# Strips of keys, a table on a 64-byte grid, first loads on two queues and a searched order in a one-core encoder layer

## The chip, the cores and the metric

The kernel runs on one core of a Trainium2 chip. The metric is device time in microseconds of one execution, as the median of several runs. The core has a matrix engine (TensorE, "PE" in the profile, whose weight loads are listed apart as "PEld"), three engines for elementwise work (VectorE "DVE", ScalarE "ACT", GpSimd "POOL") and SyncE ("SP"), which in the kernel before issues every DMA. The engines run at the same time and wait for each other by semaphores. Matmuls write into PSUM (8 banks of 128 x 512 float32), everything else lives in SBUF (128 partitions).

## The reference: what is computed

One encoder layer is applied to two sequences with the same weights: a "prompt" of 512 tokens and a "sample" of 1024 tokens, both 1024 wide, in float32. With `h = rms_norm(x)`:

```
u_pool, g_pool, q, k, v, g_attn = split(h @ w_in)          # 1024 -> 6 x 512
pool_out = pool_mixer(u_pool) * silu(g_pool)               # centred means over 2/4/8/16 tokens, 4 groups
q, k     = rms_norm per head (8 heads of 64), q / sqrt(64)
attn_out = neighbourhood_attention(q, k, v, rpb) * silu(g_attn)
y        = x + concat(pool_out, attn_out) @ w_out
```

The attention sees the tokens as a grid 64 columns wide: 16 rows in the sample, 8 in the prompt. A token attends to 8 rows by 16 columns around it, clamped at the borders; a learned bias per head depends on the row and column distance between query and key.

## The kernel before

**Numbers.** Operands of the large products are split into a high and a low part (`split`, `low`), and a product is three matmuls: high by high, high by low, low by high (`mm3`). The transposes of q, k and of the softmax weights are done on TensorE against an identity (`ident`).

**Stages.** The four pairs of heads are run one after the other, first for the sample (`ss`), then for the prompt (`pr`). For a pair p: `project_qkv` multiplies 128 tokens at a time by the pair's q, k, v columns (tile `acc`), normalises, writes v to DRAM (`vd`), and transposes q and k (bank `ptq`) into the tiles `q` and `k`, two token tiles (4 rows of the grid) at a time; `gate` and `u_block` make the gates and the input of the pooling (banks `accg`, `accu`); `attention` makes the pair's two heads; `pooling` the pool group. At the end the output projection (bank `acco`) reads the mixed activations back from DRAM, in part by a scheme with fewer products (`T`, `S`, `A`).

**Attention of the sample, before.** A head is 8 blocks of 128 queries: two halves of the grid (`rt`), 8 rows each, by four groups of 16 columns (`cb`). A block's keys are 12 rows by 32 columns, stored row by row; in the first and last column group only 24 of the 32 columns are multiplied (288 scores), in the others all (384). Per block: two matmuls make the scores (bank `s`, high and low part of k), DVE adds the bias and takes the maximum, ACT takes the exponential (`ns` or `ns_edge`), one of DVE and ACT normalises, three transposes (bank `pt`), a split into `pp`, three matmuls with v (bank `po`), and after every second block three DVE instructions and one of ACT fold the result into the gate `sg`. The bias tile is loaded from a table in DRAM (`tab`) by 13 DMAs a head, as the bias of a block depends on how its rows are clamped; v is loaded by 4 DMAs for every 4 rows, with columns that overlap between the groups. The prompt has 4 blocks a head with 8 rows of keys and two chunks.

**Order.** The program is not issued as written. Each call is recorded as an `Op`, and `Plan.order` is a list scheduler: it keeps a clock, a cost per operation (`cost`), one DMA pipe (`transfer`) and the rings of buffers, and at each moment starts on every free engine the ready operation with the lowest priority number, then the lowest sequence number. Work that waits for another engine gets `TO_PE = 800` ns on the way. Some operations may go to one of several engines (`choice`). The resulting order is fixed at build time, and each engine runs its list in that order.

**The start.** SP issues `g_sb` (the norm's weights), then x and the first weights chunk by chunk. The first projection takes four token tiles together (`group` 4 in `tok_blocks`); for chunk c of the 1024 inputs each of the four does its three matmuls.

Of the kernel before, what the change touches and what calls it, by code (L numbers as in the profile page):

```python
# [35 lines left out]
CT = (2, 1, 1, 0)  # L36
BANKS = dict(acc=3, s=2, pt=2, po=1)
# [6 lines left out]
class Plan:  # L44
# [4 lines left out]
    class Op:  # L49
        __slots__ = ("eng", "fn", "ns", "bytes", "pri", "seq", "need", "next", "alloc", "uses", "port", "half", "ways")  # L50
# [178 lines left out]
    def order(self):  # L229
        ops = self.ops  # L230
        wait = [len(op.need) for op in ops]
        for op in ops:
            for d in op.need:
                ops[d].next.append(op)
# [35 lines left out]
        while True:  # L270
            for eng, heap in ready.items():
                left_over = []
                while heap and not busy[eng]:
# [23 lines left out]
                    if op.bytes:  # L297
                        dma = max(dma, end + 650) + op.bytes
                        done = dma + 1300
                    heapq.heappush(events, (end, 0, op.seq))  # L300
# [26 lines left out]

    def issue(self):
        for _, op in self.order():
            op.fn()  # L330


TO_PE = 800
# [5 lines left out]
def encoder(ctx, tc, xn_p, xt_p, xn_s, xt_s, w_in, w_out, w_pool, pscale, ng, qg, kg,  # L339
# [23 lines left out]

    g_sb = sb.tile([P, KC], F32, name="g_sb")
    ident = sb.tile([P, P], F32, name="ident")
    qk_t = sb.tile([P, 2], F32, name="qk_t")
    gqk = sb.tile([P, 1], F32, name="gqk")
    psc = sb.tile([P, NPAIR], F32, name="psc")
    edge = sb.tile([P, NPAIR, 16], F32, name="edge")

    def late_consts():
        sp.dma_start(out=qk_t[:, 0:1], in_=qg)
        sp.dma_start(out=qk_t[:, 1:2], in_=kg)
        dve.scalar_tensor_tensor(out=gqk, in0=qk_t[:, 0:1], scalar=HD ** -0.5, in1=qk_t[:, 1:2],
                                 op0=ALU.mult, op1=ALU.mult)
        sp.dma_start(out=psc, in_=pscale)
        sp.dma_start(out=edge, in_=edge_d)

# [3 lines left out]
    tab = dram.tile([32, HR, 32], F32, name="tab")  # L382

    def build_table():
        rel = ring("pv", 1, [P, 80], "rel")
        sp.dma_start(out=rel[0:HR, 0:48], in_=rpbm.rearrange("h r c -> (h r) c"))
        sp.dma_start(out=rel[0:HR, 48:79], in_=rpb.rearrange("h r c -> (h r) c"))

# [14 lines left out]
    def bias_rows(out, h, ro, q0, nq, a):  # L403

        o = tab.offset + (h * 15 + ro) * 32
        if nq == 1:
            sp.dma_start(out=out[16 * q0:16 * q0 + 16, :, a:a + 256],
                         in_=bass.AP(tab.tensor, o, [[HR * 32, 16], [8 * HR * 32, 3], [1, 256]]))
            return
        for ct in range(3):  # L410
            sp.dma_start(out=out[16 * q0:16 * (q0 + nq), ct, a:a + 256],
                         in_=bass.AP(tab.tensor, o + ct * 8 * HR * 32, [[32, nq], [HR * 32, 16], [1, 256]]))

    def load_bias(bt, kind, h):
        if kind == "all":
            bias_rows(bt, h, 0, 0, 8, 0)
        elif kind == "top":
            bias_rows(bt, h, 3, 3, 5, 0)
            for q in range(3):
                bias_rows(bt, h, 3, q, 1, (3 - q) * 32)  # L420
        else:
            bias_rows(bt, h, 0, 0, 4, 128)
            for q in range(4, 8):
                bias_rows(bt, h, 3, q, 1, (7 - q) * 32)
# [63 lines left out]
    ns_edge = {cb: sb.tile([P, 384], F32, name=f"ns_edge_{cb}") for cb in (0, 3)}  # L488
    bias = [sb.tile([P, 3 * 384], F32, name=f"bias_{i}") for i in range(2)]
# [3 lines left out]
    class Sequence:  # L493


        def __init__(self, sq, S, kt_rows, hts, Rb):
            self.sq, self.S, self.kt_rows, self.hts, self.Rb = sq, S, kt_rows, hts, Rb
            self.NT, self.NB, self.CH, self.KEYS = S // P, S // 512, kt_rows // 4, kt_rows * 32
            self.mixed = dram.tile([KC, P, S], F32, name=f"mixed_{sq}")
            self.rr = sb.tile([P, self.NT], F32, name=f"rr_{sq}")  # L500
# [14 lines left out]

        def prep(self, raw, xt, b, c):

            sp.dma_start(out=raw, in_=xt[c * P:(c + 1) * P, b * 512:(b + 1) * 512])
            ht = self.hts[b][c]
            split(ht[:, 0], ht[:, 1], raw, g_sb[:, c:c + 1])  # L520
# [21 lines left out]
        def tok_blocks(self, accs, w, t0):  # L542
            with plan.priority(MAIN):
                for c in range(KC):
                    for t, acc in enumerate(accs, t0):
# [11 lines left out]
        def project_qkv(self, p, w, group=1):  # L557
# [3 lines left out]
            for t0 in range(0, self.NT, 2):  # L561
# [33 lines left out]
                for i, t in enumerate((t0, t0 + 1)):  # L595
# [7 lines left out]
                    pe.transpose(pt[:, i * P:(i + 1) * P], in_=qkv[:, 0:P], identity=ident)  # L603
                    pe.transpose(pt[:, 256 + i * P:256 + (i + 1) * P], in_=qkv[:, P:256], identity=ident)
# [4 lines left out]
                rt, r0 = (2 * t0) // 8, (2 * t0) % 8  # L609
                lo, hi = 7 - r0, 3 - r0  # L610
                qa = slice(base + rt * 512, base + (rt + 1) * 512)
                ka = slice(base + t0 * P, base + t0 * P + 256)
                own = [slice(hd * HD, hd * HD + HD) for hd in range(2)]
                k_src = [pt[own[hd], 256:512] for hd in range(2)]
                q_src = [pt[own[hd], 0:256].rearrange("p (r cb c) -> p r cb c", r=4, cb=4) for hd in range(2)]
                q_dst = []
                for hd in range(2):
                    for rows in (own[hd], own[1 - hd]):
                        v = q[hd][rows, qa].rearrange("p (cb r c) -> p r cb c", cb=4, r=8)
                        q_dst.append(v[:, lo::-1, :, ::-1] if hi < 0 else v[:, lo:hi:-1, :, ::-1])  # L620
                for hd in range(2):
                    for rows in (own[hd], own[1 - hd]):
                        act.activation(out=k[hd][rows, ka], in_=k_src[hd], func=AF.Copy, scale=gqk[own[hd]])
                    act.activation(out=q_dst[2 * hd], in_=q_src[hd], func=AF.Copy)
                for hd in range(2):
                    low(k[2 + hd][own[hd], ka], k_src[hd], k[hd][own[hd], ka], gqk[own[hd]])
                    low(q_dst[2 * hd + 1], q_src[hd], q_dst[2 * hd])
                rg = t0 // 2
# [15 lines left out]

        def attention(self, p):
            for hd in range(2):
                for rt in range(self.NB):
                    h = 2 * p + hd
                    kind, i = (("top", 0), ("bot", 1))[rt] if self.S == 1024 else ("all", h % 2)
                    bt = bias[i][:, 0:3 * self.KEYS].rearrange("p (t c) -> p t c", t=3)  # L650
                    load_bias(bt, kind, h)
                    self.head_rows(p, hd, rt, bt)

        def head_rows(self, p, hd, rt, bt):
            sq, KEYS, base = self.sq, self.KEYS, self.base(p)
            h, lo, rbase = 2 * p + hd, hd * HD, 4 * rt

            g = sg[lo:lo + HD, base + rt * 512:base + (rt + 1) * 512]
            for cb in range(4):
                nm = f"{sq}_{h}_{rt}_{cb}"  # L660
                s = bank("s", f"s_{nm}")
                qo = base + rt * 512 + cb * P

                c0, n = CK[cb]

                def kv(x):
                    return x[:, base:base + self.S].rearrange("p (r c) -> p r c", c=GW)[
                        :, rbase:rbase + self.kt_rows, C0[cb] + c0:C0[cb] + c0 + n]

                def seen(x):  # L670
                    return x.rearrange("p (r c) -> p r c", c=32)[:, :, c0:c0 + n]
                sv = s[:, 0:self.kt_rows * n]
# [401 lines left out]
```

## Time and profile before

| | us |
|---|---|
| median of 3 runs (lowest to highest) | 648.28 (647.86 to 649.45) |
| the profiled execution | 648.4 |
| its span, from the first to the last instruction | 646.6 |
| TensorE busy | 635.0 |
| VectorE busy | 557.1 |
| ScalarE busy | 372.8 |
| GpSimd busy | 100.6 |

A row of a group of instructions reads: line, engine, operation, output<-inputs, output and input shape, count | busy us, mean ns of one | idle time of the engine just before them and what ended it. All recorded operations carry the line of the helper that issues them, L330, so groups are told apart by the names of their tiles (s_s is the bank `s` of the sample, po_p the bank `po` of the prompt). [...]

### The profile page before, as it was taken

How to read it: one execution, taken by the hardware profiler on the slowest of the kernel's cores; microseconds unless marked ns; L12 is line 12 of the kernel's file. 1: busy time of each engine (PE TensorE's matmuls, PEld its weight loads, DVE VectorE, ACT ScalarE, POOL GpSimd, SP SyncE). 2: the span in 40 equal slices, each digit the busy share in tenths (PEclk: the TensorE clock that was granted, in tenths of full speed). 3: DMA queues.
4: the chain of work that ended last, by engine and by line, in shares of the span. 5: the costliest groups of instructions: out<-in, count | busy, mean ns of one | idle time of the engine just before them, and what ended most of it. 6: DMA issues, size and time to landing. Idle time of an engine off the chain costs nothing.

```text
span 646.6 us, 11390 instructions
## 1 busy us (share of the span) xinstructions
PE 635.0 (98%) x3404; PEld 567.0 (88%) x3404; DVE 557.1 (86%) x1647; ACT 372.8 (58%) x910; POOL 100.6 (16%) x142
## 2 busy tenths in 40 slices
PE   6999999999999999999999999999999999999997
PEld 5998899988899888999889989899899878887886
DVE  6688999899987999967999989989999989879742
ACT  5766786568656476544777556477566457323210
POOL 1130100000000000101001110021212423405412
PEclk9999999999999999999999999999999999999999
DMA  8974354442274522425344355545556687843631
GB/s 304 348 205 143 104 169 124 123 121 79 59 246 137 182 62 69 134 95 152 127 112 143 109 168 162 174 139 144 169 174 195 189 261 231 269 152 118 191 131 65
DMA packets 92961, 101.53 MB, mean 157 GB/s; under 512 B 12900, under 2 KB 78564, under 8 KB 92900
## 3 DMA queue, kind: packets, MB, share of 16 engines
q1 hardware_dynamic: 92900, 100.81, 50.7%
q8 instruction: 27, 0.44, 0.3%
q14 instruction: 34, 0.28, 0.1%
HBM read 81.41 MB, written 19.37 MB: 156 GB/s over the span
## 4 chain that ended last, share of the span: by engine, by line
PE 91%; DVE 4%; DMA 3%; issue 1%; ACT 0%; SPq 0%; DVEq 0%; ACTq 0%
PE acc_s L330 21%; PE acco L330 15%; PE accg_s L330 14%; PE acc_p L330 10%; PE accu_s L330 7%; PE accg_p L330 6%; PE po_s L330 4%; PE accu_p L330 3%; PE pt_s L330 3%; PE s_s L330 3%; DMA xr<-in_xn_s 1%; PE po_p L330 1%; PE ptq_s L330 1%; DVE B L330 1%; PE pt_p L330 1%
## 5 line engine op out<-in xcount | busy, mean ns | idle before, releaser
L330 PE MATMUL acc_s<-w_sA,ht_s 128*128 128x384 f32 x768 | 145.9, 342 | 6.3 <-DVE w_sA L330 6.3
L330 PEld LDWEIGHTS acc_s<-w_sA,ht_s 128*128 128x128 f32 x768 | 136.0, 190 | 7.6 <-ACT ht_s L330 5.9
L330 PE MATMUL accg_s<-ht_s,w_sT 128*128 128x512 f32 x384 | 100.4, 399 | 0.0
L330 PEld LDWEIGHTS accg_s<-ht_s,w_sT 128*128 128x128 f32 x384 | 70.0, 188 | 12.0
L330 PE MATMUL acc_p<-w_pA,ht_p 128*128 128x384 f32 x384 | 75.4, 339 | 0.7 <-DVE w_pA L330 0.5
L330 PEld LDWEIGHTS acc_p<-w_pA,ht_p 128*128 128x128 f32 x384 | 66.1, 188 | 1.8 <-DVE w_pA L330 0.8
L330 PE MATMUL acco<-B,left 128*128 128x512 f32 x228 | 56.2, 395 | 0.6 <-DVE left L330 0.6
L330 PE MATMUL accu_s<-ht_s,w_sT 128*128 128x512 f32 x192 | 53.0, 400 | 0.0
L330 PEld LDWEIGHTS acco<-B,left 128*128 128x128 f32 x228 | 41.9, 188 | 9.5 <-DVE left L330 1.0
L330 PE MATMUL accg_p<-ht_p,w_pT 128*128 128x512 f32 x192 | 47.6, 395 | 0.0
L330 PEld LDWEIGHTS accg_p<-ht_p,w_pT 128*128 128x128 f32 x192 | 35.3, 188 | 6.9
L330 ACT ACTIVATE k<-ptq_s,gqk 64x256 fp32r<-64x256 f32 x64 | 30.1, 470 | 18.8 <-PE ptq_s L330 18.1
L330 PEld LDWEIGHTS accu_s<-ht_s,w_sT 128*128 128x128 f32 x192 | 34.6, 188 | 5.1
L330 DVE TENSOR_TENSOR xr<-acco,xr 128x512 f32<-128x512 f32 x30 | 20.5, 686 | 20.4 <-PE acco L330 18.2
L330 ACT ACTIVATE ns_edge<-ns_edge,sm_s 128x288 f32<-128x288 f32 x54 | 28.4, 529 | 16.5 <-DVE sm_s L330 16.3
L330 ACT ACTIVATE ns_s<-ns_s,sm_s 128x384 f32<-128x384 f32 x53 | 31.7, 610 | 10.1 <-DVE sm_s L330 9.9
L330 DVE TENSOR_TENSOR pp_s<-pt_s,pp_s 128x384 fp32r<-128x384 f32 x64 | 34.5, 544 | 0.3
L330 PE MATMUL po_s<-pp_s,v 128*128 128x256 f32 x192 | 32.0, 287 | 0.0
L330 PE MATMUL s_s<-k,q 128*128 128x288 f32 (+1 forms) x128 | 31.4, 330 | 0.0
L330 PEld LDWEIGHTS po_s<-pp_s,v 128*128 128x128 f32 x192 | 28.9, 188 | 1.5
L330 POOL TENSOR_TENSOR vt_s<-qkv_s,vt_s 128x128 fp32r<-128x128 f32 x17 | 9.1, 540 | 122.0 <-ACT vt_s L330 97.3
L330 ACT ACTIVATE qkv_s<-acc_s,rr_s 128x384 f32<-128x384 f32 x24 | 13.7, 578 | 23.6 <-PE acc_s L330 20.9
(221 smaller groups left out, 1350.4 us busy)
## 6 DMA issues: line engine op xcount, KB each, us to landing
v<-vd_s SPq DMA_DIRECT2D x64, 128.0 KB
wr_sA<-in_w_in SPq DMA_DIRECT2D x32, 192.0 KB
wr_sT<-in_w_in SPq DMA_DIRECT2D x32, 192.0 KB
wr_pA<-in_w_in SPq DMA_DIRECT2D x32, 192.0 KB
wr_pT<-in_w_in SPq DMA_DIRECT2D x32, 192.0 KB
out<-xr SPq DMA_DIRECT2D x24, 256.0 KB
x<-in_xt_s SPq DMA_DIRECT2D x16, 256.0 KB
vd_s<-vt_s SPq DMA_DIRECT2D x32, 128.0 KB
```

Of the source, the lines that this page charges most:

```text
L330: op.fn()
```

## The change

- **Strips.** The sample's attention takes 8 strips of 8 columns by all 16 rows as its 128 queries. A strip's keys are 23 columns by 16 rows (368, three chunks; `KS`), in the two edge strips 16 columns (256, two chunks; `EDGE`). q and k are stored column by column, 16 rows together, so that a strip's keys are one contiguous stretch. To write them so, the transposes go against permuted identities (`by_column`), which bring the two rows of a token tile side by side; the copies then write pairs of elements, 64 bytes apart. The low part of k takes two instructions for one, and the product with the gate steps over the rows of the grid.
- **Bias table.** A second table (`tab_s`) is built for the sample: rpb is transposed on TensorE, four pairs of heads are laid out on POOL in rows of 16 float32 and stored to DRAM by 10 DMAs. A head's bias is then 3 DMAs. The prompt keeps the old table, with simpler loads.
- **v** of the sample is loaded by 8 DMAs a pair, all after the last token tiles, in tiles that alternate between pairs.
- **Tiles.** Small constants are moved or widened so that tiles behind them begin at multiples of 64 bytes; `ns` has four fixed tiles.
- **Start.** The first x is SP's first DMA; `g_sb` and the first weights go out on ACT's queue; the load of ACT's table comes behind them. Twelve matmuls of 384 columns on a constant (`IDLE`) are put ahead of the first real one. For the first chunk the four token tiles do high by high first, then low by high, then high by low.
- **Search.** `issue` calls `search` instead of `order`. It runs the list scheduler, picks one of the 14 longest modelled waits of TensorE, follows back what that operation waited for, raises the priority of some of these operations or lowers that of the ones ahead of them, and keeps the change if the modelled end comes earlier; 150 times (`SEARCH`).

```
-    def head_rows(self, p, hd, rt, bt):
...
+        def sample_block(self, p, hd, cb, bt, g):
+            first, a, n = ((0, 0, EDGE) if cb == 0 else (6, EDGE + KS, EDGE) if cb == 7 else (cb - 1, EDGE, KS))
+            ks = slice(first * P, first * P + n)
+            gv = g.rearrange("p (r cb c) -> p cb c r", r=16, cb=8)[:, cb - 1:cb + 1] if cb % 2 else None
+            self.block(p, hd, cb, q[hd][:, cb * P:(cb + 1) * P], k[hd][:, ks], k[2 + hd][:, ks], bt[:, a:a + n],
+                       ns[cb % 4], lambda x: x[:, 0:n],
+                       [vs[p % 2 * 2 + j // 4][:, j % 4] for j in range(first, first + (n + P - 1) // P)],
+                       gv, lambda x: x.rearrange("p cb (c r) -> p cb c r", c=8))
...
+                    def rows_of(x, r):
+                        return x.rearrange("p (c r) -> p c r", r=16)[:, :, r:r + 4].rearrange(
+                            "p c (i r) -> p i c r", r=2)
+
+                    def q_block(x):
+                        return rows_of(x, 12 - 2 * t0)[:, ::-1]
+
+                    def k_block(x):
+                        return rows_of(x, 2 * t0)
...
+                    for i in range(2 if self.S == 1024 else 1):
+                        low(*[x[:, i] if self.S == 1024 else x for x in (out, src, high)], gqk[own[hd]])
...
+                        for j in range(8):
+                            sa = bass.AP(vd.tensor, vd.offset + 8 * j * 256, [[256, 8], [GW * 256, 16], [1, 256]])
+                            sp.dma_start(out=vs[p % 2 * 2 + j // 4][:, j % 4].bitcast(F32), in_=sa)
...
+            for i, first, a, n in ((0, 8, 0, EDGE), (1, 0, EDGE, KS), (0, 0, EDGE + KS, EDGE)):
+                t = tab_s[i]
+                sp.dma_start(out=bt[:, a:a + n],
+                             in_=bass.AP(t.tensor, t.offset + (h * 512 + first) * 16, [[16, 8], [512, 16], [1, n]]))
...
+        for h in range(0, 8, 2):
+            t = staged(f"tab_s_{h}")
+            pool.memset(t[0:32], NEG)
+            for dst, step, src, move, n in ((56, 15, 3, 0, 9), (192, 16, 4, 1, 4), (8, 16, 0, 1, 3)):
+                pool.tensor_copy(out=at(t, dst, [256, 2], [step, n]), in_=at(rt, 15 * h + src, [15, 2], [move, n]))
+            tv = t.rearrange("p (q c) -> p q c", c=16)
+            sp.dma_start(out=tab_s[0][h:h + 2].rearrange("h q d c -> d (h q) c"), in_=tv[0:32])
+            sp.dma_start(out=tab_s[1][h:h + 2, :, 7:23].rearrange("h q d c -> d (h q) c"), in_=tv[7:23])
...
+    idle_in = vs[0][:, 0:2].rearrange("p a b -> p (a b)")
+    dve.memset(idle_in.bitcast(F32), 1.7)
+    idle = bank("po", "idle")
+    with plan.priority(FIRST):
+        for i in range(IDLE):
+            pe.matmul(idle[:, 0:BW], lhsT=idle_in[:, 0:P], rhs=idle_in[:, 0:BW], start=True, stop=True)
...
+                ss.load(x, xt_s, b, c)
+                act.dma_start(out=g_sb, in_=ng)
+                w.extend(load_w(w_in[0], BW, "sA0", (c,), act))
...
+                    if len(accs) == 4 and t0 == c == 0:
+
+                        for i, (a, b) in enumerate(((0, 0), (1, 0), (0, 1))):
+                            for t, acc in enumerate(accs):
+                                pe.matmul(acc[:, 0:BW], lhsT=self.hT(c, a, t * P, P), rhs=w[c][:, b],
+                                          start=i == 0, stop=False)
+                        continue
...
+        best = attempt()
+        for _ in range(SEARCH):
+            changes = change(best[2], best[1])
...
+            new = attempt()
+            if new is not None and new[0] < best[0]:
+                best = new
+            else:
+                for op, pri in reversed(old):
+                    op.pri = pri
+        return self.order()
```

More of the change, by code (lines that the diff above doesn't have):

```diff
@@ L49 @@
     class Op:
[L50 removed]
+        __slots__ = ("eng", "fn", "ns", "bytes", "pri", "seq", "need", "next", "alloc", "uses", "port", "half", "ways",
+                     "begin", "done")
     class Engine:
@@ L328, in issue @@
     def issue(self):
-        for _, op in self.order():
+        for _, op in self.search():
             op.fn()
+IDLE = 12
+SEARCH = 150
 TO_PE = 800
@@ L613, in project_qkv @@
-                own = [slice(hd * HD, hd * HD + HD) for hd in range(2)]
-                k_src = [pt[own[hd], 256:512] for hd in range(2)]
-                q_src = [pt[own[hd], 0:256].rearrange("p (r cb c) -> p r cb c", r=4, cb=4) for hd in range(2)]
-                q_dst = []
+                    for x, at in enumerate((i * P, 256 + i * P)):
+                        pe.transpose(pt[:, at:at + P], in_=qkv[:, x * P:(x + 1) * P],
+                                     identity=ident if self.S == 512 else by_column[x])
@@ L617, in project_qkv @@
+                q_dst = [q_block(q[hd][rows]) for hd in range(2) for rows in (own[hd], own[1 - hd])]
                 for hd in range(2):
                     for rows in (own[hd], own[1 - hd]):
[L619 to L623, printed above, removed]
+                        act.activation(out=k_block(k[hd][rows]), in_=k_src[hd], func=AF.Copy, scale=gqk[own[hd]])
@@ new lines, in attention @@
+                h = 2 * p + hd
+                bt = bias[h % 2]
+                load_bias(bt, self.S == 1024, h)
+                g = sg[hd * HD:hd * HD + HD, self.base(p):self.base(p) + self.S]
+                for cb in range(self.S // P):
+                    if self.S == 1024:
+                        self.sample_block(p, hd, cb, bt, g)
+                    else:
+                        self.prompt_block(p, hd, cb, bt, g)
+                sp.dma_start(out=self.mixed[4 + p, hd * HD:hd * HD + HD], in_=g)
@@ L779, in encoder @@
         pool.memset(k[2 + hd][HD - hd * HD:P - hd * HD].bitcast(F32), 0.0)
-    for t in ns_edge.values():
+    for t in ns:
         pool.memset(t, 0.0)
-    for bt in bias:
-        pool.memset(bt, NEG)
     for p in range(NPAIR):
@@ L819, in encoder @@
     pool.memset(U[:, 520:536], 0.0)
+    for cb in (0, 3):
+        pool.memset(ns[cb], 0.0)
     pool.memset(U[:, 1048:1056], 0.0)
```

251 lines of the change are left out of this document (153 added, 98 removed).

## The prediction

> **What bounds the kernel now.** I read the page first: the engines' shares, the granted clock, the chain of waits.
>
> ```profile
> span 646.6 us, 11390 instructions
> ...
> PE 635.0 (98%) x3404; PEld 567.0 (88%) x3404; DVE 557.1 (86%) x1647; ACT 372.8 (58%) x910; POOL 100.6 (16%) x142
> ...
> PEclk9999999999999999999999999999999999999999
> ...
> PE 91%; DVE 4%; DMA 3%; issue 1%; ACT 0%; SPq 0%; DVEq 0%; ACTq 0%
> ```
>
> TensorE is busy for all but 11.6 us of the span, and the chain that ends last runs over it for 91%. DVE is second, at 86%. A busy TensorE need not be at its peak, so next I asked what TensorE waited for:
>
> ```profile
> PE acc_s L330 <- DVE w_sA L330: 6.3, 2, 5.9
> PE acco L330 <- DVE left L330: 0.6, 1, 0.6
> PE acc_p L330 <- DVE w_pA L330: 0.5, 1, 0.5
> ```
>
> The large wait is the one for the first weights; 6.3 us of the 11.6 lie there. Later waits come to 1.1 us; nearly all the rest lies behind the last matmul. Then the chain of waits in order of time, for what one matmul costs when nothing holds it; the last five rows are the same view cut to 230 to 262 us, in the middle of a sample head pair's attention.
>
> ```profile
> 119.56 10.83 PE acc_s L330 x62
> 588.08 54.81 PE acco L330 x238
> ...
> by line: PE accu_s L330 33.9%; PE accg_s L330 27.3%; PE pt_s L330 14.3%; PE po_s L330 13.4%; PE s_s L330 11.7%
> ...
> 241.28 0.35 PE po_s L330 x3
> 243.51 0.33 PE pt_s L330 x3
> 244.07 0.36 PE s_s L330 x2
> 246.17 0.27 PE s_s L330 x2
> ```
>
> A 384-column matmul takes 10.83/62 = 0.175 us, a 512-column one 54.81/238 = 0.230. In the attention window the chain is matmuls and nothing else: softmax, splitting and loads are all hidden behind gates and pool inputs. Per instruction a value matmul (po) costs 0.117 us, a transpose (pt) 0.110, a score matmul of 384 keys 0.18 and one of 288 keys 0.135. So the sample stages are worth what TensorE's instruction stream is worth, as long as DVE keeps up. How near DVE is, by stage (columns: PE, weight loads, DVE, ACT, POOL, clock, DMA):
>
> ```profile
> 0.00:50.00 50.00, 43.70 (x230) 42.02 (x231) 35.19 (x106) 31.36 (x60) 9.85 (x24) 1.00 0.86 280
> 50.00:131.00 81.00, 81.00 (x470) 74.59 (x469) 75.59 (x255) 56.16 (x139) 5.65 (x10) 1.00 0.44 132
> 131.00:217.00 86.00, 86.00 (x487) 78.71 (x486) 75.93 (x244) 54.30 (x134) 2.64 (x6) 1.00 0.46 136
> 217.00:302.00 85.00, 85.00 (x484) 78.08 (x483) 73.33 (x223) 49.50 (x123) 5.26 (x9) 1.00 0.36 105
> ...
> 137.00:166.00 29.00, 29.00 (x174) 25.60 (x173) 28.11 (x91) 22.11 (x58) 0.00 (x0) 1.00 0.27 77
> ```
>
> One head pair of the sample takes some 86 us, of which DVE works 75.9: 10.1 us are free. While the scores are made (137 to 166) DVE is at 97%, and TensorE still never waits.
>
> **The change part by part. Strips instead of row tiles.** Blocks stay at 8 a head. Each had 12 rows by 32 columns of keys, three chunks, so 24 transposes and 24 value matmuls a head. A strip sees 23 columns by 16 rows, 368 keys and three chunks; the two edge strips see 256 and two: 6 x 3 + 2 x 2 = 22. Over 8 heads 16 transposes and 16 value matmuls go: 16 x (0.110 + 0.117) = 3.6 us. Score matmuls: from 0.135 at 288 and 0.18 at 384 a key costs 0.00047 us, so 368 keys 0.1725 and 256 keys 0.12. Before 64 x 0.18 + 64 x 0.135 = 20.2; after 96 x 0.1725 + 32 x 0.12 = 20.4: 0.2 more. The table needs one transpose more, 0.1. Replacing the identity by a permuted one changes no count. Sum **-3.3 us**, all of it on the path, since the chain there is TensorE alone.
>
> **What the strips cost DVE and ACT.** The groups that matter:
>
> ```profile
> L330 DVE SCALAR_TENSOR_TENSOR k<-ptq_s,gqk,k 64x256 fp32r<-64x256 f32 x32 | 15.4, 483 | 8.1 <-ACT q L330 7.6
> L330 DVE SCALAR_TENSOR_TENSOR st_s<-st_s 128x8 f32<-128x8 f32 x96 | 16.6, 174 | 2.0
> L330 DVE TENSOR_TENSOR q<-ptq_s,q 64x256 fp32r<-64x256 f32 x32 | 13.5, 422 | 0.6
> L330 DVE TENSOR_TENSOR sg<-pv_s,sg 64x256 f32<-64x256 f32 x32 | 13.6, 425 | 0.5
> L330 DVE TENSOR_TENSOR pp_s<-pt_s,pp_s 128x384 fp32r<-128x384 f32 x64 | 34.5, 544 | 0.3
> L330 DVE TENSOR_TENSOR pp_p<-pt_p,pp_p 128x256 fp32r<-128x256 f32 x32 | 12.9, 411 | 0.4 <-ACT pp_p L330 0.4
> ```
>
> The low part of k falls into two instructions of 128 elements. Between 174 ns at 8 elements and 483 at 256 (1.25 ns each) that is an estimated 0.324 us; per head pair 16 x 0.324 against 8 x 0.483 is +1.3 us. Bounds: 0.174 (-1.1 us) and 0.483 (+3.9). I take the middle, as width is what separates the two rows. Four edge blocks a pair split 256 columns instead of 384: 4 x (0.544 - 0.411) = -0.5. So +0.8 us a pair on DVE, hidden by the 10.1 us free behind the scores. Without that cover it would cost 4 x 0.8 = 3.2 us.
>
> What no row shows is the new addressing: q and k are written in pairs of elements 64 bytes apart, and the product with sg steps 256 bytes from element to element. The nearest rows (q, written in reversed runs of 16; sg, in runs) cost 422 and 425 for 256 elements. I take the same price, as reversed runs already change nothing between them. The other end: every such element twice as dear. That is 256 x 1.25 = 0.32 us for each of 8 q, 8 sg and 8 k (two halves), 7.7 us a pair; with 0.8 it stays under the 10.1 free, less the 0.8 by which the pair's TensorE work shrinks. Three times is 15.4, and does not fit: a rival below.
>
> [...]
>
> **Order and loads.** Scores now need all rows of q and k before the first block. Instructions on q and k, 131 to 217 us (scores on PE; copies of q and k on DVE and ACT), then three rows of the views of bias and of rel, with shortest, median and longest ns and the first and last start:
>
> ```profile
> 142.00:166.00 24.00, 6.05 (x27) 4.43 (x25) 0.67 (x2) 0.00 (x0) 0.00 (x0) 1.00 0.30 85
> 166.00:196.00 30.00, 0.08 (x1) 0.00 (x0) 0.00 (x0) 0.00 (x0) 0.00 (x0) 1.00 0.52 161
> ...
> L330 SPq DMA_DIRECT2D bias<-tab x128: 303/538/872, 42.1 to 493.7; - x128
> L330 POOL COPY tab<-rel x4: 280/360/534, 27.5 to 28.6; 120x288 f32<-120x288 f32 x1, 120x112 f32<-120x112 f32 x1, 120x256 f32<-120x256 f32 x1, 120x128 f32<-120x128 f32 x1
> L330 DVE CUSTOM_DVE_ANT_1 ns_edge<-s_s,bias x32: 426/440/459, 66.7 to 355.0; 128x288 f32<-128x288 f32 x32
> ```
>
> The last copies of k start at 141 and the first scores at 137: waiting costs the attention some 4 us of delay. The next pair overwrites q and k only at 196, 30 us after the last scores, so the delay is covered, at nothing. SP issues 80 bias, 32 v and 8 mixed loads and stores fewer and 10 for the new table more, 110 x 0.54 = 59 us of its queue; TensorE waits for none of these in the sample stages, so I count nothing. The new table: transpose, four pairs of memset and three copies (about 1.5 us a pair at 0.36 each), in two staging buffers. From 28.6 us, with 3.8 us for a store or load to land (the row of wr_sA below: issued 1.64, used 5.42), it is there by 28.6 + 1 + 2 x (3.0 + 3.8) = 43, the bias at 47; first use is 66.7. Stores in 64-byte pieces could be slower; 19 us cover them. The permuted identities are two POOL copies, under 1.1 us.
>
> **The start.** In time order, columns start, duration, engine:
>
> ```profile
> 0.74 0.38 SPq L330 DMA_DIRECT2D g_sb<-in_ng  x1
> 1.18 0.42 SPq L330 DMA_DIRECT2D x<-in_xt_s  x1
> 1.64 0.43 SPq L330 DMA_DIRECT2D wr_sA<-in_w_in  x1
> ...
> 5.42 0.36 DVE L330 CAST w_sA<-wr_sA 128x384 fp32r<-128x384 f32 x1 [4.55 <-DMA wr_sA<-in_w_in]
> ...
> 5.92 0.66 PE L330 MATMUL acc_s<-w_sA,ht_s 128*128 128x384 f32 x1 [5.92 <-DVE w_sA L330]
> ...
> 6.36 0.55 DVE L330 TENSOR_TENSOR w_sA<-wr_sA,w_sA 128x384 fp32r<-128x384 f32 x1
> ...
> 6.96 2.29 PE L330 MATMUL acc_s<-w_sA,ht_s 128*128 128x384 f32 x6 [0.38 <-DVE w_sA L330]
> ...
> 8.72 11.50 PE L330 MATMUL acc_s<-w_sA,ht_s 128*128 128x384 f32 x58
> ```
>
> The first weights are the third issue, at 1.64. With x first on SP and g_sb and the weights on ACT's queue they go at about 0.74 + 0.42 = 1.16: 0.5 us earlier, and the first matmul at 5.4. Then the tempo: the sixth matmul of the row at 6.96 is the first of the row at 8.72, so 1 + 5 + 58 = 64 matmuls run from 5.92 to 20.22; less 0.17 us by which one outlasts its successor's start, that is 14.13 us against 64 x 0.175 = 11.2. So 2.95 us are lost, in the wait for the low weights (5.92 to 6.96) and in slow matmuls right behind (five starts in 1.76 us, 0.35 each, though the granted clock reads 1.00). The diff puts 12 idle matmuls ahead, from the end of a memset (about 1.4) for 12 x 0.32 = 3.8 us, over at 5.2, and runs four matmuls on high parts alone before the low weights are wanted (ready at 6.41; the fifth row starts at 6.1 on the low x). I leave 0.15 us for the next chunk and 0.5 for matmuls still slow: 2.95 - 0.65 + 0.5 = **-2.8 us**. Bounds: 0.5 (the loads alone) and 3.45.
>
> [...]
>
> **The search** looks for an order with fewer modelled waits of TensorE. It can win the 1.1 us of listed waits; I take -0.5. The other bound is a loss: a stall like that of w_pA and the other load near 466 us, 0.5 us listed, in each of 8 head pairs, +4.
>
> Sum against the profiled execution, 648.4 us (span 646.6 and 1.8 around it): -3.3 - 2.8 - 0.5 = -6.6, so 641.8; the median of the runs, 648.28, stands 0.1 lower: **641.7 us**.
>
> **Rivals. The start's gain is given back** (chance 0.16): the work behind the first projection (the row factors, the T weights, which wait for slots) may not come earlier. For it: the DMA engines are busy for 0.86 of the first 50 us, against 0.36 to 0.46 later. Against: TensorE never waits from 6.96 to the gates. 648.3 - 3.3 - 0.5 = 644.5.
>
> **Addressing binds DVE** (0.12, slower): pair and single-element steps in q, k and sg cost more than some 2.1 times a plain element, and DVE becomes the bound of each pair. At 2.5 times it has 11.6 + 0.8 us more a pair, against 9.3 free: 3.1 us over, 12 in four pairs: 654. For it: DVE at 97% in the score window, and no row with such steps. Against: reversed runs cost nothing.
>
> **It does nothing that can be seen** (0.12): the new order's waits (4 us, as above) and the lost start together eat the gain: 648.3 - 3.3 - 0.5 + 4.5 = 649.0, within 0.3%, which is what a measurement of this kernel can tell from no change.
>
> **How the numbers follow.** The forecast keeps 0.60, with a range of its own of 640 to 644.5 from the start's and the halves' bounds. Faster is the forecast and the first rival, 0.76; same 0.12; slower 0.12. Low end: all of 3.45 and 1.1 taken, 640.4, and waits hidden in busy time besides: 638. High end 651: it takes in the first and third rival, and leaves out the DVE one.
>
> **What would show it.** Transposes and value matmuls of the sample at 176 each; idle matmuls from about 1.4 and the real ones at 0.175 from about 6; first real one near 5.4; sg and q rows still near 0.42 us; TensorE's chain unbroken from 131 on. If sg or k rows read 0.7 us and more, or TensorE waits on scores or pp by microseconds, I am wrong.

## The result

The changed kernel takes 652.19 us in the median of 7 runs (650.97 to 654.25), the kernel before beside it 648.45 (647.65 to 649.45, 7 runs): a ratio of 1.006, 95% interval 1.0044 to 1.0075. It is slower by 0.6%, some 3.7 us between the medians, where 641.7 us was forecast.

The page of the changed kernel, the first two lines that were read of the kernel before:

```profile
span 652.4 us, 11269 instructions
...
PE 640.6 (98%) x3385; PEld 564.7 (87%) x3385; DVE 564.6 (87%) x1670; ACT 369.1 (57%) x906; POOL 119.3 (18%) x178
```

TensorE does 19 matmuls and transposes fewer (3,385 with the 12 idle ones and the one for the table; 32 fewer in the strips) and is busy 5.6 us longer. The profiled execution is the slowest of the seven (654.25), so its single waits are taken as examples, not as sums. Its groups on DVE, the two on TensorE whose counts change, and TensorE's waits:

```profile
L388 DVE TENSOR_TENSOR sg<-pv_s,sg 64x256 f32<-64x256 f32 x32 | 23.6, 736 | 0.5
L388 DVE SCALAR_TENSOR_TENSOR k<-ptq_s,qk_t,k 64x128 fp32r<-64x128 f32 x64 | 22.4, 350 | 9.7 <-ACT q L388 8.3 <-ACT k L388 0.3
L388 DVE TENSOR_TENSOR q<-ptq_s,q 64x256 fp32r<-64x256 f32 x32 | 13.5, 423 | 0.5
```

```profile
L388 PE MATMUL po_s<-pp_s,v 128*128 128x256 f32 x176 | 30.7, 289 | 1.2 <-DVE pp_s L388 1.0
L388 PE MATMUL pt_s<-ident,ns 128*128 128x128 f32 x176 | 30.5, 273 | 1.4 <-ACT ns L388 1.4
```

```profile
PE pt_s L388 <- ACT ns L388: 1.4, 2, 1.1
PE po_s L388 <- DVE pp_s L388: 1.0, 3, 0.5
...
PE acc_s L388 <- ACT w_sA L388: 0.6, 1, 0.6
...
PE acc_s L388 <- DVE w_sA L388: 0.4, 1, 0.4
```

The product with the gate costs 736 ns in the mean where it cost 425. The shortest, median and longest of the 32, in the changed kernel:

```profile
L388 DVE TENSOR_TENSOR sg<-pv_s,sg x32: 641/668/1508, 88.3 to 375.6; 64x256 f32<-64x256 f32 x32
```

In the kernel before they are 398, 417 and 606; a few long ones lift the mean. TensorE now has listed waits on transposes and value matmuls of the sample (pt_s, po_s), of which the kernel before lists none. By stage (PE, weight loads, DVE, ACT, POOL, clock, DMA):

```profile
50.00:131.00 81.00, 80.27 (x457) 73.22 (x457) 75.60 (x246) 55.71 (x137) 12.00 (x20) 1.00 0.37 101
131.00:217.00 86.00, 84.65 (x472) 76.41 (x471) 75.48 (x248) 55.29 (x136) 5.04 (x9) 1.00 0.36 111
217.00:302.00 85.00, 84.54 (x470) 75.79 (x469) 74.88 (x234) 47.49 (x116) 7.64 (x12) 1.00 0.27 83
```

DVE is no busier per pair than before (75.5 of 86 us against 75.9), and yet TensorE has gaps in every stage. The listed waits do not add up to the loss. A second thing shows only in the streams that wait for nothing: 24 gate matmuls in a row, and the last 238 of the output projection.

```profile
304.91 5.73 PE L388 MATMUL accg_s<-ht_s,w_sT 128*128 128x512 f32 x24
```

```profile
593.33 55.54 PE acco L388 x238
```

The 238 took 54.81 us before; here 55.54, 3.1 ns more each: 55.54/238 = 233 ns a matmul, where the record of one lasts 393 to 395 in the mean and so outlasts its successor's start. In the kernel before the 24 take 5.67 (the row stands with the experiments on places).

### The profile page after: what moved, and what is told of

Read it like the earlier page. It is cut to its first block, busy times and chain, and to the rows that moved or that the text cites. A ratio compares the mean times of both kernels' runs of the same rounds, so it can differ in the third digit from the quotient of the medians.

```text
span 652.4 us, 11269 instructions
## 1 busy us (share of the span) xinstructions
PE 640.6 (98%) x3385; PEld 564.7 (87%) x3385; DVE 564.6 (87%) x1670; ACT 369.1 (57%) x906; POOL 119.3 (18%) x178
## 5 line engine op out<-in xcount | busy, mean ns | idle before, releaser
L388 PEld LDWEIGHTS acc_s<-w_sA,ht_s 128*128 128x128 f32 x768 | 134.2, 188 | 4.2 <-DVE ht_s L388 0.9
L388 ACT ACTIVATE ns<-ns,sm_s 128x368 f32<-128x368 f32 (+1 forms) x111 | 61.7, 576 | 33.1 <-DVE sm_s L388 32.9
L388 PE MATMUL acc_p<-w_pA,ht_p 128*128 128x384 f32 x384 | 78.8, 343 | 0.0
L388 ACT ACTIVATE k<-ptq_s,qk_t 64x256 fp32r<-64x256 f32 x64 | 30.8, 481 | 13.3 <-PE ptq_s L388 12.4
L388 DVE TENSOR_TENSOR pp_s<-pt_s,pp_s 128x384 fp32r<-128x384 f32 (+1 forms) x64 | 32.7, 514 | 0.5 <-ACT pp_s L388 0.4
L388 ACT ACTIVATE ze<-ze 128x512 f32<-128x512 f32 x24 | 15.2, 631 | 31.4 <-DVE ze L388 30.5
L388 POOL TENSOR_TENSOR vt_s<-qkv_s,vt_s 128x128 fp32r<-128x128 f32 x21 | 12.8, 614 | 109.6 <-ACT vt_s L388 54.8
L388 PE MATMUL pt_s<-ident,ns 128*128 128x128 f32 x176 | 30.5, 273 | 1.4 <-ACT ns L388 1.4
L388 PE MATMUL s_s<-k,q 128*128 128x368 f32 (+1 forms) x128 | 31.3, 330 | 0.0
L388 DVE CUSTOM_DVE_ANT_0 ns<-s_s,bias 128x368 f32<-128x368 f32 (+1 forms) x64 | 31.0, 497 | 0.1
```

## The experiments

Each ratio is against runs of the kernel before on the same chip; "before" was 648.6 to 648.9 us there. Gains in microseconds are worked out from the ratios.

**Is the searched order at fault?** The changed kernel with the plain order, and the kernel before with the search.

```
-SEARCH = 150
+SEARCH = 0
```

> The changed kernel with the search left out (0 tries): strips, table, loads and idle matmuls stay, the order is the list scheduler's first one. The changed kernel takes 652.2 us, the kernel before 648.4. Theory A (the searched order is too thin for the chip): the first order keeps the slack that the search spent, so it is no slower than 652, and near 648. Theory B (the dear product with the gate, 0.736 us instead of 0.425, and other costs of the strips): the search still helps, so without it the time is 654 to 660. Theory C (the order of loads and the late v): as B.

Measured: 661.3 us (660.46 to 661.86), ratio 1.0193 [1.0178, 1.0207]. Its first head pair and the waits of TensorE:

```profile
50.00:131.00 81.00, 76.90 (x421) 68.25 (x420) 74.22 (x253) 49.94 (x123) 6.78 (x14) 0.96 0.34 91
```

```profile
PE s_s L388 <- DVE sm_s L388: 1.8, 1, 1.8
PE s_s L388 <- DVE q L388: 1.7, 1, 1.7
```

```
-        for _, op in self.order():
+        for _, op in self.search():
```

> The kernel before with the search alone. Theory A: no gain, 648 to 652. Theory B: the search is sound where the costs are right; it wins some of the waits that are listed and hidden, 643 to 647.

Measured: 647.9 us (646.84 to 649.2), 0.9986 [0.9977, 0.9995]. The search is no cause of the loss: it takes 0.9 us off the kernel before and some 9 off the one with strips, where the plain order starts 36 TensorE instructions fewer in 50 to 131 us.

**The start alone**, put into the kernel before (first loads on two queues, twelve idle matmuls, the first chunk part by part):

```
+                act.dma_start(out=g_sb, in_=ng)
+                w.extend(load_w(w_in[0], BW, "sA0", (c,), act))
+                                pe.matmul(acc[:, 0:BW], lhsT=self.hT(c, a, t * P, P), rhs=w[c][:, b],
```

> The kernel before with the new start alone: first x on SP, g_sb and the first weights on ACT's queue, twelve idle matmuls, high parts first in the first chunk. The first real matmul at 5.7 us and the real ones fast from the start, as in the changed kernel, which is 2.0 us ahead of the kernel before at 15 us of the span. If that is kept: 646.4. If it is given back at 20 to 50 us, as in the changed kernel (level again at 50 us): 648.4.

Measured: 647.17 us (645.37 to 647.81), 0.9971 [0.9960, 0.9983]: some 1.9 us gained, and kept. If the gains of start and search added up, strips, their table and the new places of tiles would cost more than the whole difference; a run below (start and search with w at 0) shows that they need not add up.

**The price of the product, first attempt.** The changed kernel, same order; the product runs over the gate's runs of 8 side by side, and only its other input is read in steps of 16 elements (64 bytes).

```
-g.rearrange("p (r cb c) -> p cb c r", r=16, cb=8)     x.rearrange("p cb (c r) -> p cb c r", c=8)
+g.rearrange("p (r cb c) -> p cb r c", r=16, cb=8)     x.rearrange("p cb (c r) -> p cb r c", c=8)
```

> The changed kernel with one edit: the product with the gate goes over the gate's runs of 8 columns and reads pv in steps of 16 elements, instead of reading pv in a run and the gate in steps of 64 elements. Same result, same order on every engine. Theory B, if the step of 64 elements on the gate's side is what is dear: the 32 instructions fall from 0.736 to about 0.43 us, 10 us of DVE go, and of TensorE's waits behind pp, pv and ns the larger part: 646 to 649. If a step of 16 elements on one input is as dear: about 0.6 to 0.74 us and no change of time, 652. Theory A: the instructions may get cheaper, but the time stays above 650.

Measured: 653.47 us (651.73 to 654.4), 1.0067 [1.0051, 1.0082].

```profile
L388 DVE TENSOR_TENSOR sg<-pv_s,sg 64x256 f32<-64x256 f32 x32 | 21.4, 670 | 0.5
```

The mean went from 736 to 670 ns only (the median from 668 to 615), 32 x 66 ns = 2.1 us, and the time did not follow. I read this at first as clearing the product; it only shows that one input in such steps is nearly as dear as the gate in steps.

**The place of the weights.** The change merges small tiles, and the tiles of `w` come to lie 128 bytes past a multiple of 256, where they lay 192 past one; `ht` lies on multiples of 256 in both. Three kernels move only that, with every order as it was; in the second only the row sums and factors change places with the weights, in the other two the tiles that lie behind the weights move along by 64 bytes.

```
 e5 (changed kernel):       +    pad = sb.tile([P, 16], F32, name="pad")       # ahead of the weights: w at 192
 e9 (changed kernel):       rr and ss allocated behind the weights             # w at 0
 e6 (kernel before):        +    warm = gqk_w[:, 1:2]  and rr of the prompt in psc   # w at 128
```

> The changed kernel with the same order of instructions, but with the weight tiles 64 bytes further on in the partition, 192 bytes past a multiple of 256 instead of 128, where the kernel before has them (the tiles of h stay on a multiple of 256). Theory P, the place of the weights against h sets the distance from one matmul to the next: in the trace of the changed kernel some 1,320 matmuls of 512 columns start 231.8 ns apart, in the kernels built from the one before 229.6; of the 1,152 of 384 columns 176.1 against 175.0. 1,320 x 2.2 + 1,152 x 1.1 = 4.2 us, so about 648 us, and the two distances back at 229.6 and 175.0. Theory W, waits for vector work alone are the loss, and the distances come from something else: 652 us as before, distances unchanged.

Measured: 651.98 us (649.71 to 653.83), 1.0046 [1.0030, 1.0063].

> The changed kernel with the same order, the weight tiles 128 bytes lower, on a multiple of 256 bytes like the tiles of h; nothing else moves but the row sums and row factors, which lie behind the weights now. Theory P: the output projection, whose two operands both lie on multiples of 256 in every kernel, starts its 512-column matmuls 228.4 ns apart, so 1,320 x 3.4 + 1,152 x 1.1 or more = 5.7 us or more off: about 646.5 us. A rival within P, it is 64 bytes against 0 of the address by itself that counts (odd multiples of 64 good, 128 and 0 bad): 652. Theory W: 652.

Measured: 649.83 us (647.21 to 652.8), 1.0020 [1.0003, 1.0037].

> The kernel before, same order, the weight tiles 64 bytes lower, at 128 past a multiple of 256 as in the changed kernel (two small tiles of one column share a tile with others). Theory P: 4.2 us slower, about 652.7 us, with 512-column matmuls 231.8 ns and 384-column ones 176.1 ns apart. Theory W: 648.5 us as before.

Measured: 651.7 us (651.26 to 652.99), 1.0045 [1.0029, 1.0062].

The same 24 gate matmuls and the same last 238 of the output projection, in the order: kernel before (its 238 took 54.81), kernel before with w at 128, changed kernel with w at 192, with w at 0.

```profile
302.30 5.67 PE L330 MATMUL accg_s<-ht_s,w_sT 128*128 128x512 f32 x24
```

```profile
303.33 5.74 PE L330 MATMUL accg_s<-ht_s,w_sT 128*128 128x512 f32 x24
```

```profile
590.48 55.30 PE acco L330 x238
```

```profile
304.34 5.67 PE L388 MATMUL accg_s<-ht_s,w_sT 128*128 128x512 f32 x24
```

```profile
591.88 55.01 PE acco L388 x238
```

```profile
302.83 5.64 PE L388 MATMUL accg_s<-ht_s,w_sT 128*128 128x512 f32 x24
```

```profile
589.52 54.52 PE acco L388 x238
```

The place sets the distance, in both kernels and both directions: 5.74 and 5.73 with w at 128, 5.67 at 192, 5.64 at 0, and the output projection moves the same way. Over the whole trace, from all start times, as the mean from one start to the next where a matmul of the same output follows without a wait, 512 columns take about 231.7 ns at 128, 229.6 at 192 and 228.8 at 0, 384 columns 176.0, 175.1 and 174.4. The rival that 0 would be as bad as 128 falls. The output projection has a control in itself: its products with the tiles `A`, `a` and `S`, which lie in the buffers of w, start 232.1 to 233.2 ns apart with w at 128, 229.1 to 231.0 at 192 and 226.7 to 228.9 at 0, while those of `left` with `B`, whose places the move of w leaves alone, stay at 228.2 to 228.8. (The expectation of the run with w at 0 takes both operands of the output projection to lie on multiples of 256 in every kernel; `A`, `a` and `S` do not.)

In time the kernel before loses 0.45%, 2.9 us of the 4.2 expected. The changed kernel wins 2.6 us with w at 0, less than half of the 5.7 expected. With w at 192, the place that the kernel before has, it wins only some 0.9 of 4.2, a miss, and with these intervals not clear of nothing: its distances are back, its waits are not.

**Start and search with w at 0**, without strips:

> The kernel before with the new start and the search, without the strips, and the weight tiles 64 bytes further on, on a multiple of 256. The start alone gave 1.6 us and the search alone 0.9, so 646 us if the place does nothing (theory W). Theory P: another 1,320 x 1.2 = 1.6 us and whatever the 384-column ones give, so 644.5 us or less.

```
+    pad = sb.tile([P, 16], F32, name="pad")     # in the kernel before with the new start and the search
```

Measured: 648.7 us (647.69 to 650.37), 1.0000 [0.9987, 1.0013], a miss. The searched order brings a wait of its own late in the program:

```profile
PE acco L386 <- DVE sgp L386: 1.9, 1, 1.9
...
PE s_s L386 <- DVE sm_s L386: 0.6, 1, 0.6
```

So start and search, which win 1.9 and 0.9 us alone, win nothing together here.

**Start with w at 0**, plain order, no strips:

> The kernel before with the new start alone and the weights on a multiple of 256 bytes; no strips, no search. The start alone ran at 0.9971 of the kernel before; theory P takes off another 1,225 x 0.85 + 1,017 x 0.5 = 1.6 us by the distances of matmuls, so 0.9947 of the kernel before, some 645.2 us on a chip where that takes 648.6. If the place of the weights only helps where they were at 128, 0.9971 again.

Measured: 646.12 us (645.51 to 646.21), 0.9963 [0.9952, 0.9975]. Less than the 0.9947 expected. The place gives at most little here (0.9971 with w at 192, and the intervals overlap), and the plain order is better than the searched one by 0.4%, 2.4 us: about the two waits listed above.

**The price of the product, second attempt.** The changed kernel with w at 0, same order, the product written densely: the kernel leaves out putting the columns back into rows, so its result is not the layer's.

```
+                    row = sg[hd * HD:hd * HD + HD, cb // 2 * 256:cb // 2 * 256 + 256]
+                    do = partial(dve.real.tensor_tensor, out=row, in0=flat.rearrange("p s q -> p (s q)"), in1=row, op=ALU.mult)
```

> The changed kernel with the weights on a multiple of 256 bytes (the earlier run of that kind took 649.8 us, 1.002 of the kernel before), same order on every engine, but the gate's product of the sample's strips written densely, 256 columns side by side, where they are not put back into rows: the un-permutation is left out, so 32 products should cost about 411 ns (the price of the additions that read the same tile) instead of 736, 10.4 us of VectorE work less. Theory D, dear VectorE work makes the scores, the probabilities and the transposed q and k late, and TensorE waits for them: the waits of TensorE at the changes from projection to value product and to transposes (about 5 us more than without strips) shrink by half or more, 646 to 647.5 us. Theory O, the order is what is wrong and a shorter product only gives VectorE idle time: 649.5 us.

Measured: 645.78 us (644.87 to 647.49), 0.9955 [0.9941, 0.9970].

```profile
L388 DVE TENSOR_TENSOR sg<-pv_s,sg 64x256 f32<-64x256 f32 x32 | 15.4, 481 | 0.5
```

The median is 421 ns, near the 411 expected; a few long ones make the mean 481. So DVE has 32 x (736 - 481) = 8.2 us less work, and the time is 0.65% or 4.2 us less. The waits of the sample's value matmuls for pp_s (1.2 us with w at 0 before this edit) are gone from the list; that of its transposes for ns is not (1.2 us, where it was 0.6).

**Or is it the order behind the product?** The changed kernel with w at 0, the planner told 736 and 350 ns:

```
+            step, run = out.ap[-1]
+            if len(dims) > 2 and step > 1:
+                per = 2.6
+            if run == 2 and method == "scalar_tensor_tensor":
+                per = 1.74
```

> The changed kernel with the weights on a multiple of 256 bytes, the strips as they are, but the planner is told the two prices that it had wrong (the product 736 ns instead of 338, a low half of k 350 instead of 260) before it orders and searches. Theory O, the planner put the work behind these instructions as if they were cheap, so what TensorE needs came late: 646 to 647.5 us, waits before value products and transposes down by 2 to 3 us. Theory D, the work itself is too much for VectorE in a head pair: 649.5 us, no better order exists.

Measured: 651.27 us (649.96 to 652.04), 1.0043 [1.0031, 1.0055].

```profile
74.00:83.00 9.00, 4.83 (x17) 3.28 (x17) 8.81 (x19) 4.98 (x12) 0.00 (x0) 0.87 0.48 138
85.00:302.00 217.00, 217.00 (x1261) 202.41 (x1260) 196.00 (x638) 139.82 (x345) 22.29 (x30) 0.99 0.31 94
```

```profile
PE accm_s L393 <- DVE ph L393: 2.4, 1, 2.4
PE s_s L393 <- DVE q L393: 1.5, 1, 1.5
```

```profile
82.69 4.04 PE L393 MATMUL acc_s<-w_sA,ht_s 128*128 128x384 f32 x12
86.53 0.72 PE L393 MATMUL s_s<-k,q 128*128 128x256 f32 x2
```

Neither theory's time came, and the run does not decide between them. From 85 to 302 us this order has TensorE busy throughout, 1,261 instructions in 217 us (1,238 with the other order). But at 74 to 83 us DVE is at 98% (8.81 of 9.00) and TensorE waits 3.9 us for it, and behind these waits it is slow: the twelve matmuls from 82.69 to 86.53 start 0.320 us apart, where such matmuls start 0.174 apart from 87.6 us on, and the granted clock from 83 to 87 us is 0.50. The other order keeps TensorE busy from 74 to 83 (9.00 us, 48 instructions against 17), so an order without this stall exists; the plain order with strips had one like it (1.8 and 1.7 us above). In sum nothing is won.

**A cure, alone and with w at 0.** The 128 queries of a strip stand row by row inside it, by another permuted transpose and another partition order of the bias load, so that product and gate both have runs of 8.

```
-    pool.tensor_copy(out=by_column[0].rearrange("p (cb c r) -> p r cb c", cb=8, r=2),
+    pool.tensor_copy(out=by_column[0].rearrange("p (cb r c) -> p r cb c", cb=8, r=2),
-    t.offset + (h * 512 + first) * 16, [[16, 8], [512, 16], [1, n]]
+    t.offset + (h * 512 + first) * 16, [[512, 16], [16, 8], [1, n]]
```

> The changed kernel, same order and same places of all tiles (weights at 128 past a multiple of 256), only the queries of a strip stand row by row. Theory D: the product's part by itself, about 4 us off the changed kernel, 1.000 of the kernel before, about 648.5 us; with the place of the weights as the rest of the loss (another 2.5 to 3 us in the run beside this one). If the two losses are not independent (what the product frees is taken by the slower matmuls), 650 us and more.

Measured: 649.41 us (648.33 to 650.42), 1.0007 [0.9997, 1.0018].

> The whole change (strips, start, search), weights on a multiple of 256 bytes, same order on every engine as the run with the weights there that took 1.002 of the kernel before, but the 128 queries of a strip stand row by row inside it (8 columns side by side) instead of column by column: the permuted transpose of q, the partitions of the bias load and the writes of q change, and the product reads and writes runs of 8 on both sides, nothing is left out. Theory D (the dear product is what TensorE waits for): a product near 425 ns, as in the kernel before, and 645 to 646.5 us, 0.9955 of the kernel before, as with the dense product. Rival: runs of 8 are as dear as the steps of 16 on one input alone (670 ns in the run with the rows looped over), then 649.5 us.

Measured: 646.62 us (644.41 to 647.37), 0.9959 [0.9943, 0.9975].

With w at 128: the product's row, all that the list of waits has left of scores and of q and k (pt_s and po_s are not in it), and one stage:

```profile
L388 DVE TENSOR_TENSOR sg<-pv_s,sg 64x256 f32<-64x256 f32 x32 | 15.4, 482 | 0.5
```

```profile
PE s_p L388 <- DVE q L388: 0.3, 1, 0.3
PE ptq_s L388 <- DVE qkv_s L388: 0.2, 1, 0.2
```

```profile
131.00:217.00 86.00, 85.77 (x479) 77.78 (x479) 75.25 (x253) 56.07 (x139) 4.81 (x9) 1.00 0.37 115
```

The order is the changed kernel's on every engine; from 131 to 217 us 479 TensorE instructions stand where 472 stood, and from 217 to 302 us 477 where 470 stood. The product's median is 422 ns in both cured kernels, and q still costs 422. The four corners, as ratios to the kernel before:

| | w at 128 | w at 0 |
|---|---|---|
| product in steps of 256 bytes | 1.0060 | 1.0020 |
| queries row by row | 1.0007 | 0.9959 |

The product is worth 0.53 and 0.61% (3.4 and 4.0 us), the place (128 against 0) 0.40 and 0.48% (2.6 and 3.1 us). Within the intervals, some 0.1 to 0.2% each way, they add up. The dense product, which changes nothing else, gives the product the same price (4.2 us). The whole change with both cured, 0.9959, stands with the dense but incomplete product (0.9955) and with the start alone at w at 0 (0.9963); both beat the kernel before, and neither can be told from the other.

## Why the prediction was wrong

**What bounds the kernel** held: TensorE at 98%, DVE second at 87%.

**Strips, -3.3 us of TensorE work.** The counts came as said, 176 transposes and 176 value matmuls. In the totals the gain does not show: even cured, the kernel with strips (0.9959) is not faster than the one with the start and the same place of the weights but no strips (0.9963). In the traces it does. All matmuls of the first projection and all of the prompt's, with their first and last start, in the start alone with w at 0 and in the cured kernel with w at 0:

```profile
L330 PE MATMUL acc_s<-w_sA,ht_s x192: 334/334/659, 6.2 to 41.8; 128*128 128x384 f32 x192
```

```profile
L330 PE MATMUL acc_p<-w_pA,ht_p x384: 331/334/459, 346.9 to 490.5; 128*128 128x384 f32 x192
```

```profile
L388 PE MATMUL acc_s<-w_sA,ht_s x192: 331/334/689, 7.1 to 43.5; 128*128 128x384 f32 x192
```

```profile
L388 PE MATMUL acc_p<-w_pA,ht_p x384: 331/334/427, 345.8 to 490.4; 128*128 128x384 f32 x192
```

From the end of the first projection to the start of the prompt's, where the strips work, the two take 305.1 and 302.3 us; the five kernels without strips that have w at 192 or 0 lie between 305.1 and 306.7. With w at 128 the kernel before takes 307.0, the cured one 303.4. The kernels with strips put some 0.7 us more of the sample's TensorE work off behind that stretch (an estimate from the instructions that start later, at the prices of the prediction). That leaves 2.1 to 3.7 us for the strips, about the 3.3 forecast. Each figure is from one execution.

The dear product takes it all back: the same stretch is 307.8 us in the changed kernel, 4.4 more than cured, and 306.4 with w at 0, 4.1 more. In the totals the cured kernel with w at 0 loses its lead over the start alone at both ends: its first projection is over 1.7 us later, and from the prompt's start to the end it takes 1.8 us longer. Against the kernel with start and search and no strips (1.0000) it wins 2.7 us, but that kernel has the wait of 1.9 us that its own order made. So neither total alone gives the strips' price.

In the cured kernel with w at 0 the largest listed wait of the attention is 1.4 us for an exponential on ACT:

```profile
PE pt_s L388 <- ACT ns L388: 1.4, 1, 1.4
```

In the changed kernel the wait of this kind is at 186 us, where ACT stands behind a load for the prompt (columns start, duration):

```profile
185.08 0.63 ACT L388 ACTIVATE xh_p<-xh_p 128x512 f32<-128x512 f32 x1 [1.55 <-DMA xh_p<-in_xn_p]
...
185.71 0.49 ACT L388 ACTIVATE ns<-ns,sm_s 128x256 f32<-128x256 f32 x1
...
186.26 0.44 PE L388 MATMUL pt_s<-ident,ns 128*128 128x128 f32 x2 [1.13 <-ACT ns L388]
```

What makes the two ends longer was not settled.

**What the strips cost DVE: the step that failed first.** The halves of k were estimated at 0.324 us and read 0.350; q was taken at 0.42 and reads 0.423. The product was taken at 0.42, with "twice as dear" as the other end; its mean is 0.736, 1.73 times the old one (its median 1.60 times), inside that bound and past the mark of 0.7 that the prediction set itself. Wrong was what I did with the bound: "stays under the 10.1 free", hence hidden, at nothing. The free time of a pair was an average. DVE keeps 10.5 us free from 131 to 217 us in the changed kernel too, but the product stands in its queue ahead of the splits that the next value matmuls need. One such place in the changed kernel (start, duration):

```profile
369.15 0.67 DVE L388 TENSOR_TENSOR sg<-pv_s,sg 64x256 f32<-64x256 f32 x1
...
370.18 0.55 DVE L388 TENSOR_TENSOR pp_s<-pt_s,pp_s 128x384 fp32r<-128x384 f32 x1
...
370.88 0.59 PE L388 MATMUL po_s<-pp_s,v 128*128 128x256 f32 x3 [0.51 <-DVE pp_s L388]
```

In the cured kernel with w at 128 the same product takes 0.42 us, the split starts 0.79 us behind the product's start instead of 1.03, and no wait of po_s is listed. Over the whole program 8.2 us less of DVE work gave 3.4 to 4.2 us of time. The rival that DVE binds was set at a price of 2.1 times plain and more; it cost earlier and less than that, without DVE being full over a pair. Of the new addressing the traces show a price for the product: 736 ns in the mean against 425 with the gate in single elements 256 bytes apart, and 670 with one input in single elements 64 bytes apart. They show none for q, written in pairs of elements 64 bytes apart: 423 against 422. For the halves of k, also in pairs, they show nothing either way, as their 0.350 us has no row of the same width to stand against. Why the product is dear and q is not, no run shows.

**Tiles: the step that was missing.** The prediction counted nothing for the moved tiles, though the change lists them. They moved the weights by 64 bytes against h, from 192 to 128, and matmuls of 512 columns from 229.5 to 231.8 ns. That move costs the kernel before 2.9 us; undone in the changed kernel it gave 0.9, not clear of nothing. (The 2.6 and 3.1 us of the four corners are for 128 against 0, a place that neither kernel has.) No row of before could have given that price; that a part of the change had none should have been said.

**The start, -2.8.** Alone it is worth 1.9 us. In the changed kernel the idle matmuls begin and end as said, the first real one comes at 5.71 (said: 5.4), and the real ones run without a wait from 7.31 (said: at 0.175 from about 6). How far TensorE is, in the kernel before, the changed one, and the start alone with w at 0:

```profile
0.00:20.00 20.00, 13.70 (x64) 1.00 0.91 321
```

```profile
1.45 3.86 PE L388 MATMUL idle<-v 128*128 128x384 f32 x12 [1.45 <-DVE warm L388]
5.71 0.97 PE L388 MATMUL acc_s<-w_sA,ht_s 128*128 128x384 f32 x4 [0.40 <-ACT ht_s L388]
7.31 12.32 PE L388 MATMUL acc_s<-w_sA,ht_s 128*128 128x384 f32 x68 [0.63 <-DVE ht_s L388]
```

```profile
0.00:20.00 20.00, 17.16 (x84) 1.00 0.89 314
```

```profile
0.00:20.00 20.00, 18.01 (x80) 1.00 0.91 329
```

Less the twelve idle ones, TensorE has started 64, 72 and 68 matmuls by 20 us, and 93, 95 and 97 by 25. The changed kernel's lead of 8 (8 x 0.175 = 1.4 us) is down to 2 by 25 us, behind the two waits for w_sA listed above; the DMA engines are full at that time in all three (0.97 to 1.05). The last matmul of the first projection starts at 42.7 us before and at 42.5 in the changed kernel: 0.2 us of the 2.8 are left. In the seven traces with the changed kernel's order that matmul starts between 41.7 and 43.5 us, with the start alone at 41.5 and, with w at 0, 41.8. That is the first rival, the start's gain given back, and it came true there. Whether the order of loads or ACT's work at 15 to 21 us takes it was not separated.

The -2.8 counts on the idle matmuls to end the slow matmuls of the start; that was the author's estimate, which no row of the kernel before shows, and the runs bear it out only in part. In the changed kernel's trace they start 0.320 us apart up to 4.5 us and 0.17 from 4.8 on, ahead of the first real one. But in four of the twelve traces with idle matmuls, the one with the start alone and w at 0 among them, the matmuls are still 0.32 us apart up to 10.2 to 10.6 us, nearly as long as without idle ones (10.8 to 11.5). What sets the moment, no run shows.

**The search, -0.5**: 0.9 us on the kernel before, right in size. That it would decide whether strips cost 4 or 12 us was not foreseen, nor that it can lose (1.0000 against 0.9963 with start and place alike, 2.4 us, of which one wait is 1.9).

**Order and loads** held: in the changed kernel no wait of TensorE for the table, for v or for the sample's later scores is listed.

So the step that failed is the product with the gate, hidden and put at nothing: it costs 3.4 to 4.0 us, though DVE was not full over a pair. Beside it the place of the weights was not in the sum (2.9 us by the kernel before, 0.9 by the changed kernel), and of the start's -2.8 some 2.6 were given back. Between forecast and result lie 10.5 us (-6.6 to +3.9 by the ratio); these terms come to 8.9 to 9.5 of them with the larger price of the place, to 6.9 to 7.5 with the smaller. The rest stays open.

## What to carry to other kernels

Free time of a second engine per stage is no cover for an instruction that stands, in order, ahead of what the first engine needs next: cost it on the path when the engine is as busy as DVE was here, at 88% (10.5 of 86 us free, and yet 3.4 to 4.0 us lost). Look at both sides of an elementwise instruction for single elements far apart (668 and 615 ns here against 422 in runs), and turn the order where a transpose is being paid for anyway. When a change moves tiles, compare streams of matmuls that wait for nothing before and after (229.6 and 231.7 ns here), and try their places as an experiment of its own. Two orders of the same work differed here by 2.4 us, as much as the parts of the change: so measure a part between two moments of the program too, and not by the total alone.

## What the runs showed of the hardware

The distance between matmuls changed with the place in the partition of the operand from the buffers of w, which is the stationary one at 512 columns and the moving one at 384. As a mean over all those of 512 columns it was 228.8 ns with w on a multiple of 256 bytes, 229.6 with w at 192 past one, 231.7 at 128; at 384 columns 174.4, 175.1 and 176.0. Only these three places were tried, and no run shows why.

The DVE product of 64 x 256 elements took 422 ns in the median in runs of 8, 615 with one input in single elements 64 bytes apart, 668 with the gate in steps of 256 bytes. The means, 482, 670 and 736, hold a few of 0.8 to 1.5 us.

And in two runs the granted clock is below 1.00 around waits of TensorE. In the kernel with the told planner, behind waits of 1.5 and 2.4 us, the granted clock is 0.50 from 83 to 87 us, and matmuls of 384 columns start 0.320 us apart instead of 0.174. In the kernel without search the granted clock is 0.96 over the first pair, where two waits of 1.8 and 1.7 us stand.
